# Two-block transformer kernel: 48 modulation units of block 1 leave TensorE and become sums over row tiles on ScalarE, VectorE and GpSimd

## The chip, the core and the metric

The kernel runs on one core of one Trainium2 chip. The metric is the device time of one execution in microseconds (us); the median of three runs is compared. The engines are TensorE (PE; its weight loads are listed as PEld), VectorE (DVE), ScalarE (ACT), GpSimd (POOL) and SyncE (SP), whose queue here only issues the DMAs of the weight stream. Each engine takes its instructions in one fixed order and waits at the first one whose inputs or buffers are not ready.

## The reference

A sequence of 256 tokens with 1024 features passes a first block of two layers (attention, then a gated delta net, each followed by a swiglu feed-forward part) and a second block of two layers. Each layer of the first block is steered by six vectors of 1024 numbers, a vector-matrix product with a weight of its own:

```
cond = jax.nn.silu(c)
for layer in range(DEPTH):
    mod = (cond @ ada_w[layer] + ada_b[layer])[:, None, :]
    shift_m, scale_m, gate_m, shift_f, scale_f, gate_f = jnp.split(mod, 6, axis=-1)
    h = rmsnorm(x, norm_mix_g[layer]) * (1.0 + scale_m) + shift_m
    ...  # mixed = attention (layer 0) or gated delta net (layer 1) of h
    x = x + gate_m * mixed
    h = rmsnorm(x, norm_ffn_g[layer]) * (1.0 + scale_f) + shift_f
    x = x + gate_f * swiglu(h, ffn_w_in[layer], ffn_w_out[layer])
```

The second block has nine such vectors per layer, for two condition vectors (its weight is called `w_mod` in the kernel). "Chunk (l, ch)" below is vector ch of layer l of the first block: 0 and 1 are shift and scale of the mixer, 2 its gate, 3 and 4 shift and scale of the feed-forward part, 5 its gate.

## The kernel before

**The stream.** All weights come through one list of 785 units, `PLAN`, each a tile of 128 rows with up to 1024 columns (512 KB). SP's queue issues their loads in that order, at most 12 units ahead (`pump`). 545 units are matrix weights ("mats"): they land in one of 6 raw buffers, ACT rounds them to a high part (L393), DVE takes the rest as a low part (L394), and PE multiplies both. A product of fp32 data is three matmuls, L420 to L422. With 256 tokens a mat is 24 matmuls.

**The modulation.** The other 240 units are modulation rows: a chunk is eight units (`kt` 0 to 7) of 128 rows each, in a pool of only three buffers, `rawm`. There are two ways to use a unit (`mod_unit`):

- "mod": four small matmuls with the condition as stationary operand (L516, eight instructions in the trace), added up in PSUM over the eight units.
- "acc": the unit, scaled row by row by the condition, is added to a [128, 1024] tile `macc`. Unit 0 is a scaled copy on ACT (L503); every other unit either a multiply-add on DVE (L510) or, in phases which have a tile `mprod`, a scaled copy on ACT into `mprod` (L507) and an add on GpSimd (L508). When all eight are in, `settle` sums `macc` over the partitions with the same four small matmuls.

Both ways end in `mod_end`: a copy on ACT (L533), two transposes on PE (L536), an add on DVE (L544).

**The order.** A scheduler fixes each engine's order at build time, from the program's order and its own estimates; nothing is reordered on the chip. The phases run one after the other: `attn`, `ffn1` (FFN 0), `gdn` (the gated delta net), `ffn1` again (FFN 1), and then the second block. Each phase has its own tiles (`PHASES`). In the feed-forward phases `macc` has two buffers, in `attn` one.

**Entering the gated delta net.** The norm of the new x runs `rsq` (ACT L479, DVE L570 to L572), then for each of eight tiles a multiply on DVE (L639), the high part on ACT (L640) and the low part on DVE (L641). PE then multiplies them, beginning with the mats `ab`, q and k of head 0; each projected head passes a convolution on DVE (L978, out of PSUM). Later four heads at a time go through a triangular inverse, whose tiles `dec` and `m` GpSimd masks (L1025, L1056).

**Which units go which way.** Before the change, of the first block's chunks (0,0) and (0,1) are "mod" units ahead of everything, (0,2) and (0,3) are "acc" units among the attention's mats, (1,0) and (1,1) "acc" units among FFN 0's mats. (0,4), (0,5) are "mod" units between the attention's output mats and behind them, (1,2), (1,3), (1,4) "mod" units among the delta net's mats, and (1,5) stands as eight "mod" units ahead of FFN 1.

Of the kernel before, what the change touches and what calls it, by code (L numbers as in the profile page):

```python
# [12 lines left out]
AF = mybir.ActivationFunctionType  # L13
OP = mybir.AluOpType
AX = mybir.AxisListType

T = 256
# [11 lines left out]

# ---------------------------------------------------------------- weight stream  # L30
# A unit is a [128, n] tile of weights, n <= 1024, made of blocks
# (array, leading index, first row, first column, width).

# [13 lines left out]
def _spread(units, mods, every):  # L47
    """The modulation units one by one between the others: the first three at once."""
    out, mods = mods[:3], mods[3:]
    for i, u in enumerate(units):  # L50
        out.append(u)
        if i % every == every - 1 and mods:
            out.append(mods.pop(0))
    return out + mods


def _evenly(units, mods, a, b, kind="acc"):
    """The modulation units evenly between the units a to b from the end."""
    n = len(units) - a - b
    out, k = [], 0  # L60
    for i, u in enumerate(units):
        out.append(u)
        while k < len(mods) and i >= a + k * n // len(mods):
            out.append((kind,) + mods[k][1:])
            k += 1
    return out
# [30 lines left out]
def plan():  # L97
# [15 lines left out]
    u += _evenly(q, A(0, 2, 3), 4, 0)  # L113
    q = []
# [4 lines left out]
    u += _spread(q, A(0, 4, 5), 1)  # L119
    u += _evenly(_ffn_units(("f", 0), "ffn_w_in", "ffn_w_out", 0), A(1, 0, 1), MODS_IN, MODS_OUT)  # L120
# [6 lines left out]
    u += _evenly(q, A(1, 2, 3, 4), 0, 4, "mod")  # L127
    u += A(1, 5)
    u += _evenly(_ffn_units(("f", 1), "ffn_w_in", "ffn_w_out", 1), B(0, 1, 0), MODS_IN, 2 * MODS_OUT)
# [43 lines left out]
# ---------------------------------------------------------------- small vectors and constants  # L173
# [48 lines left out]
def constants():  # L222
    """Masks, rotations, the DFT and the axial rotation tables: functions of the shapes alone."""
# [66 lines left out]
class Unit:  # L290
    def __init__(self, hi, lo):
# [3 lines left out]
# Tiles of each phase: tag -> (columns, buffers)  # L295
# [3 lines left out]
    "ffn1": {"hb": (KT * 520, 1), "t": (256, 3), "s": (256, 4), "hid": (512, 11), "macc": (1024, 2), "mprod": (1024, 1)},  # L299
# [12 lines left out]
class Builder:  # L312
# [26 lines left out]
    # ---- tiles  # L339
# [34 lines left out]
    # ---- weights  # L374
# [32 lines left out]
    def flush(self, n=len(PLAN)):  # L407
        """The modulation units that stand next in the stream, up to n."""
        end = self.pos + n
        while self.pos < min(end, len(PLAN)) and PLAN[self.pos][0] != "mat":  # L410
            self.pump()
            r = self.raw.pop(self.pos)
            self.mod_unit(PLAN[self.pos][1], r, PLAN[self.pos][0] == "acc")
            self.pos += 1

    def mm3(self, out, u, j, ah, al, start, stop, w=128):
        """out += W[:, block j]^T a"""
# [6 lines left out]
    def mmt(self, out, ah, al, u, j, start, stop, w=512):  # L424
        """out += a^T W[:, block j]"""
# [6 lines left out]
    def gemm(self, u, h, c0, c1, p=None):  # L432
        """One 128-feature tile of a product over the tiles of h, columns c0..c1."""
# [6 lines left out]
    def lead(self, units, h, c0, c1):  # L440
        """The same for some units at once, tile by tile of h as they come."""
# [7 lines left out]
    def pair(self, tag, n):  # L449
        """The two parts of an operand, in one tile or two."""  # L450
# [5 lines left out]
    def split(self, src, hi, lo):  # L456
        """hi + lo = src, each exact in one pass."""
# [4 lines left out]
    def table(self, name):  # L462
        """The scalar engine's table set from here on, in the order of the program."""
# [7 lines left out]
    def after(self, i, j):  # L471
        """Instruction i goes to its engine's queue behind j."""
# [3 lines left out]
    def act(self, out, src, func, **k):  # L476
        """A function of the scalar engine that needs a table."""
# [5 lines left out]
    # ---- modulation  # L483
    def mod_unit(self, key, r, acc):
        """One tile of rows of a modulation's product with the conditions: on the tensor engine, or summed
        over the tiles by a vector engine, so that the tensor engine only sums over the partitions."""
# [13 lines left out]
        for s, a in enumerate(self.macc):  # L500
# [4 lines left out]
            if ns == 1 and "mprod" in self.tags:  # L505
                t = self.t("mprod")
                self.nc.scalar.activation(t, r, AF.Copy, scale=w)  # L507
                self.nc.gpsimd.tensor_tensor(a, a, t, op=OP.add)  # L508
# [10 lines left out]
    def settle(self):  # L519
        """The sums over the partitions that are due."""  # L520
# [30 lines left out]
    def gain(self, name, l, gname, ch):  # L551
        """g * (1 + scale), per stream."""
# [9 lines left out]
    # ---- norms  # L562
    def rsq(self, ss, inv, eps=EPS):
        """(ss * inv + eps) ** -0.5 on [128, 256], one Newton step after the tables' value."""
# [10 lines left out]
    def stats(self, total=KT, gains=None):  # L575
        """Sums of squares of total tiles. With gains, a column offset: of x and, in place of stream 1,
        of x times its gain."""
        return {"gains": gains, "acc": None, "first": {}, "n": {}, "total": total, "p": {}}

    def push(self, st, src, c0, c1):  # L580
        """Squares of one more tile, columns c0..c1. Only the last tile's own sum waits for that tile."""
# [27 lines left out]
    def enter(self, st, ns, A, B, lead):  # L609
        """h = x * r * A + B, split, stream by stream; lead starts on each stream as it is ready."""  # L610
# [9 lines left out]
    def enter_raw(self, st, A, B):  # L620
        """r, and for each tile of x the parts of x * A with those of B as more columns (an even number): of a product over
        them, the columns times r plus the last one are the product over x * r * A + B."""
# [27 lines left out]
    def project_out(self, units, src, ns, gate, st, tail=True):  # L650
        """x += gate * W^T src, tile by tile; the last tiles stream by stream, so that the norm of one
        stream runs beside the products of the other. With one stream, the first tiles at once, so that the
        last of src has time to arrive."""
# [16 lines left out]
    # ---- swiglu  # L670
    def ffn(self, key, st, ns, A, B, gate, more, before_last=None):
        """x += gate * swiglu(x * r * A + B); returns the sums of squares of the new x."""
# [53 lines left out]
    # ---- block 1, layer 0: softmax heads and stick-breaking heads  # L726
# [26 lines left out]
    def vproj(self, key, h):  # L753
        """Values with tokens on the partitions: two tiles [128, 512]."""
# [16 lines left out]
    def headsplit(self, src):  # L771
        """A tile of two heads' rows, each head in its own copy with zeros for the other."""
# [5 lines left out]
    def av(self, pt, v, hp):  # L778
        """Output rows of a pair of heads from their weights [k, (k0 q0, k0 q1, k1 q1)]."""
# [34 lines left out]
    def softmax_rows(self, s, na, scale, P):  # L814
        """P = softmax(scale * s) over the last axis of s [128, na, n]."""
# [49 lines left out]
    def sb_scores(self, qkv, hp):  # L865
        """z = masked scores, e = softplus(z), keys on the partitions."""
# [15 lines left out]
    def sb_weights(self, z, e):  # L882
        """z <- exp(z - what the keys from this one on have taken)."""
# [11 lines left out]
    def scale(self, st, A):  # L895
        """x * r * A, in the columns beside x."""
# [4 lines left out]
    def shift(self, B):  # L901
        """What scale left, plus B, split."""
# [37 lines left out]
    # ---- block 1, layer 1: gated delta rule, the whole sequence as two blocks of 128  # L940
    def gdn_gates(self, h):
        nc = self.nc
        p = self.gemm(self.get(("ab",)), h, 0, T)
        z, e, g = self.t("ga"), self.t("ga"), self.t("ga")
# [36 lines left out]
    def gdn_proj(self, heads, h, out):  # L981
        """Projections of some heads, convolved; a step for each."""
# [24 lines left out]
    def gdn_mats(self, hd, qk, v):  # L1007
        """at, lt [128 s, 3, 128 t]: q k^T and beta k k^T, transposed, with their decays (the first masked
# [583 lines left out]
```

## Time and profile before

| | before |
|---|---|
| device time, median of 3 runs | 2563.02 us (2561.24 to 2563.8) |
| profiled execution, span of the core | 2561.5 us |
| PE busy | 2501.8 us, 98% |
| DVE busy | 1689.1 us, 66% |
| ACT busy | 1128.5 us, 44% |
| POOL busy | 195.9 us, 8% |
| data moved by DMA | 408.38 MB, 159 GB/s mean |

The profiled execution lies inside the range of the timed runs, and its time is its span. The first block takes about the first 745 us of it. Shares of busy time are means over stages with different limits. A matmul's listed duration overlaps the next one's, so the distance between two starts tells what a matmul costs in a stream.

### The profile page before, as it was taken

Reading aid. Unit: us, or ns where it says so; the run is one execution under the profiler, and the core shown is the slowest. Engines: PE = TensorE matmul, PEld = TensorE weight load, DVE = VectorE, ACT = ScalarE, POOL = GpSimd, SP = SyncE. Lnnn points to the kernel's source line nnn. Section 1 sums busy time; section 2 is a strip of 40 time slices with the busy share of each in tenths; the row PEclk is TensorE's granted clock in tenths of the full one; section 3 lists DMA queues with packets and bytes.
Section 4 is the critical chain, followed back from the end, with each engine's and each line's share of the span. In section 5 each row is a group of like instructions: output and inputs, shape, how many; then the busy total and the mean of one; then the engine's idle time right before and its main releaser. Section 6 shows DMA issues by size and latency. Waiting matters only on the chain.

```text
span 2561.5 us, 39957 instructions
## 1 busy us (share of the span) xinstructions
PE 2501.8 (98%) x15915; PEld 2177.1 (85%) x15915; DVE 1689.1 (66%) x2607; ACT 1128.5 (44%) x1955; POOL 195.9 (8%) x183
## 2 busy tenths in 40 slices
PE   6999999999999999999999999999999999999998
PEld 5878998988999887878886888888888888888998
DVE  6857768765887957774646474565656565675665
ACT  4556456565645523233525432323432323555544
POOL 1004100423000100001000100000100000101000
PEclk9999999999999999999999999999999999999999
DMA  8767656324875545663220243454244453232553
GB/s 333 268 209 244 212 188 208 116 83 158 286 248 181 189 160 188 187 197 124 79 79 26 70 154 110 146 175 144 91 159 162 150 178 122 92 109 83 190 183 97
DMA packets 117402, 408.38 MB, mean 159 GB/s; under 512 B 13024, under 2 KB 16352, under 8 KB 117216
## 3 DMA queue, kind: packets, MB, share of 16 engines
q1 hardware_dynamic: 114192, 403.08, 47.8%
q10 hardware_dynamic: 3024, 2.75, 0.4%
q8 instruction: 125, 2.05, 0.3%
q14 instruction: 61, 0.50, 0.1%
HBM read 404.74 MB, written 1.05 MB: 158 GB/s over the span
## 4 chain that ended last, share of the span: by engine, by line
PE 93%; DVE 3%; DMA 2%; ACT 1%; issue 1%; POOL 0%; ACTq 0%; DVEq 0%; SPq 0%
PE pmm L420 25%; PE pmm L422 25%; PE pmm L421 25%; PE pmd L516 2%; PE pax L1389 2%; PE pax L1072 2%; PE pmm L1375 1%; DMA r<-w 1%; PE pax L421 1%; PE pax L422 1%; PE pax L420 1%; PE pax L1385 1%; DVE l L394 1%; PE pnm L607 1%; PE pmm L429 0%
## 5 line engine op out<-in xcount | busy, mean ns | idle before, releaser
L393 ACT CAST h<-r 128x1024 fp32r<-128x1024 f32 (+3 forms) x545 | 550.2, 1016 | 1025.5 <-PE pmm L421 937.6
L394 DVE TENSOR_TENSOR l<-r,h 128x1024 fp32r<-128x1024 f32 (+3 forms) x545 | 658.6, 1213 | 306.0 <-ACT h L393 296.1
L420 PE MATMUL pmm<-h,h 128*128 128x512 f32 (+1 forms) x1928 | 674.3, 351 | 6.7 <-ACT h L640 2.3
L421 PE MATMUL pmm<-h,h 128*128 128x512 f32 (+1 forms) x1928 | 669.1, 348 | 2.0 <-DVE h L641 1.9
L422 PE MATMUL pmm<-h,l 128*128 128x512 f32 (+1 forms) x1928 | 668.9, 347 | 1.0 <-DVE l L394 1.0
L420 PEld LDWEIGHTS pmm<-h,h 128*128 128x128 f32 x1928 | 365.3, 190 | 64.4 <-issue 9.3
L421 PEld LDWEIGHTS pmm<-h,h 128*128 128x128 f32 x1928 | 365.5, 190 | 49.6 <-DVE h L641 3.2
L422 PEld LDWEIGHTS pmm<-h,l 128*128 128x128 f32 x1928 | 365.3, 190 | 47.6 <-DVE l L394 1.5
L420 PE MATMUL pmm<-hid,h 128*128 128x256 f32 (+1 forms) x1053 | 349.5, 332 | 0.0
L422 PE MATMUL pmm<-hid,l 128*128 128x256 f32 (+1 forms) x1053 | 347.5, 330 | 0.3 <-DVE l L394 0.3
L421 PE MATMUL pmm<-hid,h 128*128 128x256 f32 (+1 forms) x1053 | 347.4, 330 | 0.0
L510 DVE SCALAR_TENSOR_TENSOR macc<-r,cond,macc 128x1024 f32<-128x1024 f32 x266 | 330.0, 1281 | 0.3 <-DMA r<-w 0.2
L420 PE MATMUL pmm<-hb,h 128*128 128x258 f32 x1008 | 287.3, 285 | 7.0 <-DVE s L681 6.4
L422 PE MATMUL pmm<-hb,l 128*128 128x258 f32 x1008 | 285.8, 284 | 0.0
L421 PE MATMUL pmm<-hb,h 128*128 128x258 f32 x1008 | 285.3, 283 | 0.0
L420 PEld LDWEIGHTS pmm<-hid,h 128*128 128x128 f32 x1053 | 200.1, 190 | 20.3 <-ACT h L393 1.2
L422 PEld LDWEIGHTS pmm<-hid,l 128*128 128x128 f32 x1053 | 200.1, 190 | 18.7 <-DVE l L394 0.5
L421 PEld LDWEIGHTS pmm<-hid,h 128*128 128x128 f32 x1053 | 200.1, 190 | 18.2
L647 DVE SCALAR_TENSOR_TENSOR x<-pmm,mod_w_mod,x 128x256 f32<-128x256 f32 x188 | 84.6, 480 | 176.5 <-PE pmm L422 176.2
L420 PEld LDWEIGHTS pmm<-hb,h 128*128 128x128 f32 x1008 | 191.6, 190 | 9.8 <-DVE s L681 7.2
L422 PEld LDWEIGHTS pmm<-hb,l 128*128 128x128 f32 x1008 | 192.4, 191 | 0.4 <-issue 0.4
L421 PEld LDWEIGHTS pmm<-hb,h 128*128 128x128 f32 x1008 | 192.4, 191 | 0.3 <-DVE hb L630 0.2
(337 smaller groups left out, 2891.7 us busy)
## 6 DMA issues: line engine op xcount, KB each, us to landing
r<-w SPq DMA_DIRECT2D x665, 512.0 KB, 4.3
r<-w SPq DMA_DIRECT2D x96, 448.0 KB, 3.3
r<-w SPq DMA_DIRECT2D x16, 256.0 KB, 3.0
r<-w SPq DMA_DIRECT2D x8, 384.0 KB, 3.4
const<-const SPq DMA_DIRECT2D x2, 960.0 KB, 6.1
x<-xT ACTq DMA_DIRECT2D x8, 128.0 KB, 4.6
x<-ctxT ACTq DMA_DIRECT2D x8, 128.0 KB, 3.4
out<-x ACTq DMA_DIRECT2D x4, 128.0 KB, 2.1
```

The lines of the kernel that those rows point to most:

```text
L393: nc.scalar.copy(h[:, :n], r[:, :n])
L394: nc.vector.tensor_tensor(lo[:, :n], r[:, :n], h[:, :n].bitcast(F32), op=OP.subtract)
L420: nc.tensor.matmul(out, wh, ah, start=start, stop=False)
L421: nc.tensor.matmul(out, wh, al, start=False, stop=False)
L422: nc.tensor.matmul(out, wl, ah, start=False, stop=stop)
L510: self.nc.vector.scalar_tensor_tensor(a, r, w, a, op0=OP.mult, op1=OP.add)
L516: self.nc.tensor.matmul(p[32 * g:32 * g + 32, :256], w, r[:, 256 * g:256 * g + 256], start=start, stop=stop)
L607: nc.tensor.matmul(p, self.ones, s[:, cg], start=tot == 1, stop=True)
L647: self.nc.vector.scalar_tensor_tensor(v, p[:, s * T - c0:s * T + T - c0], gate[:, 8 * s + m:8 * s + m + 1], v, op0=OP.mult, op1=OP.add)
L1072: nc.tensor.matmul(p[:, s], a[:, s], b[:, s], start=True, stop=True)
L1375: self.nc.tensor.matmul(s, q, k, start=True, stop=True)
L1389: nc.tensor.matmul(o, V[b], pt[:, 128 * b:128 * b + 128], start=b == 0, stop=b == nb - 1)
```

## The change

48 units change from "mod" to "acc": the chunks (0,4), (0,5), (1,2), (1,3), (1,4), (1,5). In the first block 16 "mod" units stay (the two chunks at the start) and 80 are "acc". The positions move with them: (0,2), (0,3), (0,4) stand one behind each mat over the attention's projections and first output mats, (0,5) among the first 16 mats of FFN 0, (1,0) and (1,1) behind those, (1,2) to (1,4) at the same places among the delta net's mats, (1,5) among the first 16 mats of FFN 1, and the first two chunks of the second block a little closer together behind those. From the second block on the order is the same.

The sum for one condition vector is also done in another way in every phase: units 2, 4 and 6 on DVE (L498 of the changed kernel), units 1, 3, 5 and 7 scaled in place on ACT (L495) and added on GpSimd (L496). `mprod` is gone; in the `gdn` phase three tiles are given up for one `macc`. On balance 384 matmul instructions of L516 go and 48 come (six more `settle`); DVE has 16 multiply-adds of 1024 columns more, GpSimd 26 adds more (40 instead of 14), ACT 6 first copies and 26 scalings more.

```
-    u += _evenly(q, A(0, 2, 3), 4, 0)
-    q = []
...
-    u += _spread(q, A(0, 4, 5), 1)
-    u += _evenly(_ffn_units(("f", 0), "ffn_w_in", "ffn_w_out", 0), A(1, 0, 1), MODS_IN, MODS_OUT)
+    u += _evenly(q, A(0, 2, 3, 4), 4, 4)
+    q = _ffn_units(("f", 0), "ffn_w_in", "ffn_w_out", 0)
+    u += _evenly(q[:16], A(0, 5), 2, 3) + _evenly(q[16:], A(1, 0, 1), 0, MODS_OUT)
...
-    u += _evenly(q, A(1, 2, 3, 4), 0, 4, "mod")
-    u += A(1, 5)
-    u += _evenly(_ffn_units(("f", 1), "ffn_w_in", "ffn_w_out", 1), B(0, 1, 0), MODS_IN, 2 * MODS_OUT)
+    u += _evenly(q, A(1, 2, 3, 4), 0, 4)
+    q = _ffn_units(("f", 1), "ffn_w_in", "ffn_w_out", 1)
+    u += _evenly(q[:16], A(1, 5), 2, 3) + _evenly(q[16:], B(0, 1, 0), 0, 2 * MODS_OUT)
...
-            "vb": (256, 4), "dec": (384, 2), "kb": (256, 1), "m": (512, 2), "dt": (512, 3), "d": (512, 2),
-            "y": (512, 2), "uu": (512, 2), "os": (512, 4), "ga": (256, 3)},
+            "y": (512, 2), "uu": (512, 2), "os": (512, 4), "macc": (1024, 1)},
...
-            if ns == 1 and "mprod" in self.tags:
-                t = self.t("mprod")
-                self.nc.scalar.activation(t, r, AF.Copy, scale=w)
-                self.nc.gpsimd.tensor_tensor(a, a, t, op=OP.add)
+            if ns == 1 and kt % 2:
+                self.nc.scalar.activation(r, r, AF.Copy, scale=w)
+                self.nc.gpsimd.tensor_tensor(a, a, r, op=OP.add)
```

The places in the engines' order at which the change is followed below are all at the entry of the delta net.

DVE before, from the end of the chunk (1,1) to the first part of the norm's output (`a` and `r` are the norm's row factor, `t` the first tile of x times it):

```order
L544 TENSOR_TENSOR mod_ada_w_1_4448<-pmd_4445,cols 128x8
L558 SCALAR_TENSOR_TENSOR gain_ada_w_1_4450<-mod_ada_w_1_4448,cols 128x8
L570 TENSOR_TENSOR a_4462<-y_4461 128x256
L571 SCALAR_TENSOR_TENSOR a_4462<-pnm_4431,a_4462 128x256
L572 SCALAR_TENSOR_TENSOR r_4460<-a_4462,r_4460 128x256
L639 SCALAR_TENSOR_TENSOR t_4469<-x_136,gain_ada_w_1_4450,r_4460 128x256
```

DVE after the change, the same place (L558, L559, L560, L627 are the norm's lines now; `r_4230` is unit 2 of chunk (1,2)):

```order
L532 TENSOR_TENSOR mod_ada_w_1_4406<-pmd_4403,cols 128x8
L546 SCALAR_TENSOR_TENSOR gain_ada_w_1_4408<-mod_ada_w_1_4406,cols 128x8
L558 TENSOR_TENSOR a_4420<-y_4419 128x256
L498 SCALAR_TENSOR_TENSOR macc_4523<-r_4230,cond,macc_4523 128x1024
L559 SCALAR_TENSOR_TENSOR a_4420<-pnm_4389,a_4420 128x256
L560 SCALAR_TENSOR_TENSOR r_4418<-a_4420,r_4418 128x256
L627 SCALAR_TENSOR_TENSOR t_4427<-x_136,gain_ada_w_1_4408,r_4418 128x256
```

A multiply-add of the modulation now stands inside the norm's chain. Units 4 and 6 of the same chunk stand further down, ahead of the low parts of the fifth and of the seventh tile (rows not shown).

ACT after the change, behind it (`h_4410` to `h_4417` are the high parts of the eight tiles; `r_4326`, `r_4564` and `r_4717` are units 3, 5 and 7 of chunk (1,2), `h_4599` is the split of a mat); before the change the eight L640 stood in one row with nothing between them:

```order
L492 ACTIVATE macc_4523<-r_4059,cond 128x1024
L468 ACTIVATE y_4419<-pnm_4389,eps1e-06_152 128x256
L468 ACTIVATE y_4419<-y_4419 128x256
L557 ACTIVATE r_4418<-y_4419 128x256
L628 ACTIVATE h_4410<-t_4427,mod_ada_w_0_3358 128x256
L628 ACTIVATE h_4411<-t_4431,mod_ada_w_0_3358 128x256
L495 ACTIVATE r_4326<-r_4326,cond 128x1024
...
L628 ACTIVATE h_4415<-t_4447,mod_ada_w_0_3358 128x256
L495 ACTIVATE r_4564<-r_4564,cond 128x1024
L628 ACTIVATE h_4416<-t_4451,mod_ada_w_0_3358 128x256
L628 ACTIVATE h_4417<-t_4455,mod_ada_w_0_3358 128x256
L495 ACTIVATE r_4717<-r_4717,cond 128x1024
L382 CAST h_4599<-r_4294 128x1024
```

Three scalings that wait for a load now stand among the high parts and ahead of the next split.

PE after the change, where the sums of chunk (1,2) are settled (`pmm_4566` is the last of the first three mats `ab`, q, k of the delta net, `pmm_4603` the fourth); 72 rows lie between the transposes that end chunk (1,1) and this `settle`:

```order
L409 MATMUL pmm_4566<-h_4417,h_4461 128x256
L410 MATMUL pmm_4566<-h_4417,h_4461 128x256
L411 MATMUL pmm_4566<-h_4417,l_4462 128x256
L504 MATMUL pmd_5420<-macc_4523,pick 32x256 x4
L409 MATMUL pmm_4603<-h_4410,h_4519 128x256
```

Before the change three "mod" units stood ahead of these three mats and the others behind them; now PE passes to the fourth mat only when the sum of all eight units is complete. The `settle` of (0,4) stands in the same way 73 rows behind that of (0,3), and that of (1,4) 85 rows behind that of (1,3).

## Rows read from the trace of the kernel before

**Rows 1.** The page, part 1: engine, busy us (share of the span), instructions.

```profile
PE 2501.8 (98%) x15915; PEld 2177.1 (85%) x15915; DVE 1689.1 (66%) x2607; ACT 1128.5 (44%) x1955; POOL 195.9 (8%) x183
```

**Rows 2.** The page, part 4: the chain that ended last, by engine.

```profile
PE 93%; DVE 3%; DMA 2%; ACT 1%; issue 1%; POOL 0%; ACTq 0%; DVEq 0%; SPq 0%
```

**Rows 3.** Timeline of PE: start, us, engine, line, operation, tiles, count [idle before].

```profile
170.77 0.28 PE L422 MATMUL pmm<-og,l 128*128 128x256 f32 x1
170.98 0.64 PE L516 MATMUL pmd<-r,cond 128*32 128x256 f32 x8
171.55 0.38 PE L420 MATMUL pmm<-og,h 128*128 128x256 f32 x1
171.77 0.28 PE L421 MATMUL pmm<-og,h 128*128 128x256 f32 x1
171.89 0.28 PE L422 MATMUL pmm<-og,l 128*128 128x256 f32 x1
```

**Rows 4.** Groups of the modulation's tile on PE, 95 to 760 us: min/median/max ns.

```profile
L516 PE MATMUL pmd<-r,cond x384: 379/379/403, 139.0 to 652.8; 128*32 128x256 f32 x192
```

**Rows 5.** Waits of PE from 100 to 700 us: us in total, times, longest.

```profile
PE pmm L420 <- DVE s L681: 6.4, 2, 5.6
PE pmd L516 <- DMA r<-w: 2.7, 2, 1.5
```

**Rows 6.** Windows: length, busy us of PE, PEld, DVE, ACT, POOL; clock, DMA share, GB/s.

```profile
200.00:235.00 35.00, 28.61 (x221) 28.15 (x220) 32.64 (x36) 20.68 (x37) 12.96 (x5) 0.90 0.68 236
...
220.00:225.00 5.00, 0.54 (x2) 0.55 (x3) 5.00 (x5) 2.42 (x5) 2.85 (x1) 0.67 0.87 281
225.00:230.00 5.00, 5.00 (x31) 5.00 (x30) 3.16 (x6) 2.02 (x4) 0.00 (x0) 0.64 0.73 278
230.00:235.00 5.00, 5.00 (x45) 5.00 (x44) 4.49 (x4) 3.27 (x7) 2.39 (x1) 1.00 0.90 346
...
403.00:440.00 37.00, 36.92 (x310) 33.77 (x308) 31.41 (x51) 23.86 (x37) 0.00 (x0) 1.00 0.74 242
440.00:456.00 16.00, 16.00 (x134) 13.88 (x130) 14.17 (x40) 15.47 (x38) 0.97 (x1) 1.00 0.21 67
```

**Rows 7.** Timeline of DVE in FFN 0.

```profile
210.07 1.21 DVE L394 TENSOR_TENSOR l<-r,h 128x1024 fp32r<-128x1024 f32 x1
...
211.54 0.41 DVE L681 TENSOR_TENSOR s<-pmm,r 128x256 f32<-128x256 f32 x1
211.87 3.38 DVE L394 TENSOR_TENSOR l<-r,h 128x1024 fp32r<-128x1024 f32 x1
215.18 0.41 DVE L681 TENSOR_TENSOR s<-pmm,r 128x256 f32<-128x256 f32 x1
```

**Rows 8.** Timeline of POOL in FFN 0.

```profile
211.77 2.39 POOL L508 TENSOR_TENSOR macc<-macc,mprod 128x1024 f32<-128x1024 f32 x1 [1.91 <-ACT mprod L507]
```

**Rows 9.** Groups of the modulation's sums, whole span: min/median/max ns, first and last start.

```profile
L508 POOL TENSOR_TENSOR macc<-macc,mprod x14: 2384/2409/3214, 193.6 to 263.6; 128x1024 f32<-128x1024 f32 x14
...
L503 ACT ACTIVATE macc<-r,cond x40: 1133/1150/1179, 40.8 to 2108.9; 128x1024 f32<-128x1024 f32 x40
...
L510 DVE SCALAR_TENSOR_TENSOR macc<-r,cond,macc x266: 1270/1278/1760, 48.3 to 2130.8; 128x1024 f32<-128x1024 f32 x133
```

**Rows 10.** The page, part 6: DMA issues, KB each, median us to landing.

```profile
r<-w SPq DMA_DIRECT2D x665, 512.0 KB, 4.3
```

**Rows 11.** Timeline of PE at the entry of the delta net.

```profile
389.72 1.50 PE L516 MATMUL pmd<-r,cond 128*32 128x256 f32 x24 [0.26 <-DVE mod_ada_w L544]
392.69 0.62 PE L420 MATMUL pmm<-h,h 128*128 128x256 f32 x3 [1.47 <-ACT h L640]
```

**Rows 12.** Timeline of ACT at the same entry.

```profile
388.60 0.37 ACT L533 COPY meada_w<-pmd 128x256 f32<-128x256 f32 x1 [0.52 <-PE pmd L516]
```

**Rows 13.** Timeline of DVE at the same entry.

```profile
390.62 0.42 DVE L571 SCALAR_TENSOR_TENSOR a<-pnm,a 128x256 f32<-128x256 f32 x1
...
398.25 0.89 DVE L641 SCALAR_TENSOR_TENSOR h<-t,mod_ada_w,h 128x256 fp32r<-128x256 f32 x2 [0.18 <-ACT h L640]
```

More of the change, by code (lines that the diff above doesn't have):

```diff
@@ L44, in _rows @@
     return ("mat", key, [(name, l, k * 128, m * 128, 128) for k in range(k0, k1)])
[L47 to L54, printed above, removed]
 def _evenly(units, mods, a, b, kind="acc"):
@@ L298 @@
              "macc": (1024, 1), "sm": (512, 2), "e": (768, 1), "pt": (768, 1), "tab": (512, 1), "t": (256, 2)},
-    "ffn1": {"hb": (KT * 520, 1), "t": (256, 3), "s": (256, 4), "hid": (512, 11), "macc": (1024, 2), "mprod": (1024, 1)},
[2 rows of a table removed]
+    "ffn1": {"hb": (KT * 520, 1), "t": (256, 3), "s": (256, 4), "hid": (512, 11), "macc": (1024, 2)},
[2 rows of a table added]
             "vb": (256, 4), "dec": (384, 2), "kb": (256, 1), "m": (512, 2), "dt": (512, 3), "d": (512, 2),
[1 row of a table removed]
[1 row of a table added]
     "mix": {"h": (512, 18), "t": (256, 2), "raw": (512, 6), "tmp": (512, 4), "o": (512, 8), "pt": (512, 4), "ru": (256, 1)},
@@ L943, in gdn_gates @@
         p = self.gemm(self.get(("ab",)), h, 0, T)
-        z, e, g = self.t("ga"), self.t("ga"), self.t("ga")
+        z, e, g = self.t("vb"), self.t("vb"), self.t("vb")
         dt, al = COLS["dt"][0], COLS["a_log"][0]
```

4 rows, old and new, of the table PHASES are left out of this document.

## The prediction

> **What bounds the kernel now.** The page's first part says it: PE is busy 98% of the span, DVE 66%, POOL 8% [rows 1]. The chain that ended last is PE's work for 93% of its length [rows 2]. So time is won by taking instructions from PE, as long as no other engine makes it wait. The modulation units are such instructions, and the timeline of PE gives their price. Of the stream of matmuls with 256 columns, one starts every 0.12 us (171.77 to 171.89). Between the L422 that starts at 170.77 and the L421 at 171.77 stand one unit and two steps of the stream, so the unit costs 1.00 - 0.24 = 0.76 us [rows 3]. All 48 units that move lie between 139 and 653 us (384 instructions) [rows 4].
>
> Then the waits. In the stretch that the change touches PE waits little: 6.4 us for the scaled products of FFN 0 (5.6 of it at once) and 2.7 us for units that had not landed [rows 5]. The 5.6 us cost more than their length: in the windows the granted clock is 0.67 while PE waits and 0.64 in the next five us, where PE starts 31 matmuls and not 45, about 1.7 us lost, and full again after 230 [rows 6]. Of TensorE's two levels, 1.2 and 2.4 GHz, it had the lower one for most of that stretch, after standing still.
>
> Last, the engines that receive the work. DVE's timeline in FFN 0 shows a split L394 of 1.21 us, and one of 3.38 us [rows 7]. The long one began 0.10 us after a GpSimd add of 2.39 us had [rows 8]. It lost 2.17 us, that is, it ran when the add was over. L681 beside it reads PSUM and stayed at 0.41 us.
>
> **What goes.** 48 units at 0.76 us are 36.5 us. Nine of them earn nothing: three groups of three stand where PE waits for a norm anyway. At the delta net's entry PE does 24 instructions and still waits 1.47 us for the first part of h [rows 11]; the other two groups are at 178 and at 638 us. That takes 6.8 us off. Six new sums over partitions (settle) are the same four matmuls and cost 6 x 0.76 = 4.6 us. Copy, transposes and bias stay. Net: -25.1 us. PE's waits for units (2.7 us [rows 5]) go with the units that were loaded in a burst: -2.7. The same burst held up the mats' loads ahead of FFN 0, and the splits, then stretched by adds, were late until 224 us. Wait and clock are 5.6 + 1.7 = 7.3 us. Now no burst is there, but the first sixteen mats of FFN 0 carry four adds and three multiply-adds of chunk (0,5), where before DVE was 32.6 of 35 us busy [rows 6]. Between nothing and 7.3 I take half: -4.
>
> **What comes, where it waits.** An "acc" chunk is a chain, since every step writes macc: one copy on ACT (1.15), four adds (2.41 each) and three multiply-adds (1.28) [rows 9], 14.6 us, and units 3 to 7 must first be loaded into a buffer that an earlier unit has left, 4.3 us from issue [rows 10], the odd ones also scaled (taken as the copy's 1.15).
>
> I follow it at the delta net's entry. The copy of chunk (1,1) ends at 388.97 [rows 12]; behind it ACT does unit 0, to 390.1; the add of unit 1 ends at 392.5, unit 2 on DVE at 393.8. That multiply-add stands in DVE's queue ahead of the norm's second step, which ran at 390.62 before [rows 13]: **the whole entry is 3.2 us late**. Unit 3: its buffer is free at 390.1, landed 394.4, scaled 395.6, added 398.0. Unit 4: done 399.3. Unit 5: free 393.8, landed 398.1, scaled 399.3, added 401.7. Unit 6: free 398.0, landed 402.3, done 403.6; behind it on DVE stand the last two low parts, ready at 404.5 where they were at 399.1. Unit 7: free 399.3, landed 403.6, scaled 404.8, added 407.2. Only then can PE settle and go on to its fourth mat. Before, its 72 matmuls from 392.69 on [rows 11] took 8.6 us, to 401.3 if nothing waited. So PE is 6 us late, not a mere 4.6 us of instructions. The lower bound is the 3.2 us, the upper 6 plus one more landing, 10.3, if unit loads queue on SP behind mats. I take 6, and 2 for the clock after the gap (nearest row: the 1.7 above).
>
> The same chain is 407.2 - 388.6 = 18.6 us from a settle to the next where a chunk follows in the same buffer. (0,4) has 73 matmuls of PE in that time, 36 of them with 512 columns: at 0.24, 0.12 and 0.06 us by their columns, some 11.5 us. The bounds are 0 (PE waits there for attention weights as well, so that time passes anyway) and 7; I take 5. (1,4) has 85 matmuls, some 8 us, but between links of the triangular inverse, which spread them out: between 0 and 10.6, I take 3. The three settles together: 16 us with the clock.
>
> **What comes, in DVE's time.** In 403 to 456 us DVE is busy 45.6 of 53 us and PE 52.9 [rows 6]; PE loses some eight units, 6 us. DVE gains three multiply-adds (3.8 us) and meets four adds. They can block it 4 x 2.17 = 8.7 us, or nothing if they always fall beside convolutions, which read PSUM; the two ends are 49.4 and 58.1 us, against 47 for PE. Half blocked, DVE needs 53.7. As splits run ahead during the wait at the settle, I take 4 us, and 2 for FFN 1's first mats, where (1,5) puts four more adds. In the attention DVE has room. ACT at 44% [rows 1] costs by order alone, which is counted above.
>
> The Trainium skill, SBUF — State Buffer, section "Who interferes with whom", says that a VectorE instruction with two inputs in SBUF and a GpSimd instruction that reads SBUF exclude each other for the whole instruction, and that one with at most one SBUF input goes free. Rows 7 and 8 agree, 3.38 beside 0.41 us. By it all adds that meet a split cost it the full length; the rival on blocking below is what that would make.
>
> **The sum.** -25.1 - 2.7 - 4 + 16 + 6 = -9.8 us. The profiled span is 2561.5, and its time is 1.5 below the median of the three runs, 2563.0. Against the median: **2553 us**.
>
> **Rivals.** *All of it is won.* Nothing waits longer at a settle, and DVE keeps up: -25.1 - 2.7 - 4 = -31.8, about 2531 us. For it speaks that DVE is at 66% [rows 1]; against it the chain just followed, made of measured durations. Chance 0.15.
>
> *Blocking eats it.* Every add costs a split its 2.17 us where DVE is nearly full. In the delta net DVE then needs 58.1 - 47 = 11 us more than PE (7 above my 4), FFN 0 keeps its late splits (4), FFN 1 loses 2 more: -9.8 + 13 = +3.2, about 2566, no change that can be told. It decides where more than half of the adds meet a split. Chance 0.17.
>
> *Slower: loads at the head of SP's queue.* A chunk's load waits on SP until a buffer is given back by ACT, POOL or DVE, and mats queue behind it; a chunk's load issued late delays the chain by one landing, and there are two links of buffers in it (unit 3 for unit 0's, then unit 6 for unit 3's). If each costs 4.3 us more at each of the three settles, 26 us are added: -9.8 + 26 = +16, about 2579. It decides from 3.3 us per settle on. For it: SP has one queue, and three buffers for such units. Against: mats are loaded far ahead, and the page's DMA rows show a median of 4.3 us, waits for the queue aside. Chance 0.23, together with smaller sums above +5 us.
>
> **How the numbers follow.** My forecast, -5 to -18 us (2545 to 2558), has 0.45. 0.2% is 5.1 us, about what a measurement of this kernel can tell from no change. Faster by more: 0.45 + 0.15 and some of the boundary cases lost, 0.58; within: 0.18; slower: 0.24. The range leaves out the far half of the first rival and the far half of the last: 2534 to 2572.
>
> **What would show it.** Right: L504 with the condition is gone after 100 us; the norm's second step at the delta net's entry starts some 3 us later behind its copy, and PE stands still ahead of the settle of (1,2); shorter gaps ahead of those of (0,4) and (1,4); the clock falls behind the longest gap; adds on POOL in pairs with splits near 3.4 us; the second block unchanged to 0.1%. Wrong: no gap ahead of the three settles (then the chain is shorter than I make it, and the first rival holds), waits of PE for L383 in 400 to 460 us longer than at the settle (the second), or SP's loads of mats landing after PE wants them (the third).

## The result and the profile after

The changed kernel is slower: 2582.31 us (median of four runs, 2581.09 to 2583.81) beside 2562.90, a ratio of 1.0076 with a 95% interval of 1.0062 to 1.0090, some 19.4 us. The forecast was 2553 us, faster, and its range ended at 2572; both are wrong. Where a run of before is compared below, it ran on the same chip as the experiment. Experiments are also compared with each other across chips; the medians of the kernel before lie between 2562.8 and 2564.1 us on them, so a difference of a us or two between such runs tells nothing.

The page's first part and the chain by engine of the changed kernel:

```profile
span 2582.0 us, 39454 instructions
PE 2487.2 (96%) x15579; PEld 2179.5 (84%) x15579; DVE 1736.9 (67%) x2623; ACT 1159.3 (45%) x1987; POOL 258.8 (10%) x209
...
PE 84%; DVE 7%; issue 3%; ACT 2%; DMA 2%; POOL 1%; DVEq 0%; SPq 0%; ACTq 0%; POOLq 0%
```

PE has 14.6 us less work than in [rows 1], in a span 20.5 us longer. The chain passes through DVE for 7% and not 3% [rows 2]. PE's waits from 100 to 700 us, us in total, times, longest, are a new list; the two rows of [rows 5] shrank or are gone:

```profile
PE pax L1021 <- DVE kb L1018: 8.0, 3, 4.5
PE pmm L409 <- ACT h L628: 7.1, 2, 6.4
PE pnm L595 <- DVE a L559: 5.5, 3, 2.2
PE pmm L409 <- DVE s L669: 4.7, 6, 1.5
PE pmm L409 <- ACT hb L617: 3.0, 2, 1.9
```

They name the norm at the delta net's entry (L628), the normalization of its heads (L559), the heads' matrices that are built ahead of the inverse (L1018) and FFN 0 and 1. None is a settle.

The stages tell more than the sum. Each starts with the first matmul of its kind in PE's timeline (attention scores, scaled products of an FFN, projections of the delta net):

| stage, us | before | after | forecast of the change | measured |
|---|---|---|---|---|
| to the first attention scores | 127.0 | 136.3 | 0 | +9.3 |
| to FFN 0 | 54.7 | 47.7 | about -2 | -7.0 |
| FFN 0 and the delta net's entry | 211.1 | 210.8 | about -4 | -0.3 |
| delta net, to FFN 1 | 247.8 | 263.9 | about -2 | +16.1 |
| FFN 1 and all behind it | 1921.0 | 1923.4 | about -2 | +2.4 |

The forecast column puts the terms of the prediction's sum into the stages where the units and settles stand in the two timelines. The settle of (0,4), at 149.7 us, is in the second row with its 5 us; of the 6 us that PE was to be late at the settle of (1,2), 3.2 are in the third row.

Most of the loss is PE standing still in the delta net: of its 263.9 us PE is busy 238.6, where it was 244.2 of 247.8. So it stands still for 25.3 us and not 3.6.

The entry of the delta net, where the prediction followed the chain step by step. First DVE, then GpSimd (start, us, engine, line, operation):

```profile
389.71 1.85 DVE L558 TENSOR_TENSOR a<-y 128x256 f32<-128x256 f32 x1 [1.00 <-ACT y L468]
391.49 1.27 DVE L498 SCALAR_TENSOR_TENSOR macc<-r,cond,macc 128x1024 f32<-128x1024 f32 x1
392.69 0.41 DVE L559 SCALAR_TENSOR_TENSOR a<-pnm,a 128x256 f32<-128x256 f32 x1
...
396.59 2.71 DVE L629 SCALAR_TENSOR_TENSOR h<-t,mod_ada_w,h 128x256 fp32r<-128x256 f32 x2 [0.18 <-ACT h L628]
...
402.00 2.99 DVE L627 SCALAR_TENSOR_TENSOR t<-x,gain_ada_w,r 128x256 f32<-128x256 f32 x2
404.92 1.27 DVE L498 SCALAR_TENSOR_TENSOR macc<-r,cond,macc 128x1024 f32<-128x1024 f32 x1
406.12 0.87 DVE L629 SCALAR_TENSOR_TENSOR h<-t,mod_ada_w,h 128x256 fp32r<-128x256 f32 x2
```

```profile
388.95 2.34 POOL L496 TENSOR_TENSOR macc<-macc,r 128x1024 f32<-128x1024 f32 x1 [5.51 <-ACT macc L492]
396.21 2.41 POOL L496 TENSOR_TENSOR macc<-macc,r 128x1024 f32<-128x1024 f32 x1 [4.93 <-ACT r L495]
401.75 2.57 POOL L496 TENSOR_TENSOR macc<-macc,r 128x1024 f32<-128x1024 f32 x1 [3.13 <-DVE h L629]
406.66 2.59 POOL L496 TENSOR_TENSOR macc<-macc,r 128x1024 f32<-128x1024 f32 x1 [2.34 <-DVE h L629]
```

As forecast, the multiply-add stands ahead of the norm's second step. That step starts at 392.69 and the last low part ends at 407.0, where it was 390.62 and 399.1 [rows 13], though everything ahead ended 1.1 us earlier. So the step is 3.2 us late, as forecast, and the low part 9.0 us, where 5.4 were forecast. Not forecast: the first three of these adds also hold up the norm's own steps beside them. L558 takes 1.85 us, where the same step (L570) took 0.43, and pairs that took 0.89 and 0.88 us take 2.71 and 2.99. Then PE, at the head of the projections and at the settle:

```profile
394.75 0.80 PE L409 MATMUL pmm<-h,h 128*128 128x256 f32 x2 [6.44 <-ACT h L628]
...
409.31 0.64 PE L504 MATMUL pmd<-macc,pick 128*32 128x256 f32 x8
```

PE stands still for the norm, and the settle itself waits for nothing. With this gap of 6.44 us the granted clock falls: it is 0.62 in 390 to 400 and 0.86 and 0.83 in the next two windows of 10 us. From 395 to 402 us PE starts a matmul of 256 columns every 0.21 us and not every 0.12: it has the lower of its two levels, 1.2 and 2.4 GHz. Some 45 us into the stage DVE is full, and PE waits for what it does next; windows of busy us (PE, PEld, DVE, ACT, POOL; clock):

```profile
440.00:450.00 10.00, 9.96 (x77) 9.55 (x76) 10.00 (x13) 6.06 (x10) 2.38 (x1) 1.00 0.82 269
450.00:460.00 10.00, 6.11 (x44) 5.51 (x44) 9.79 (x20) 9.98 (x22) 2.40 (x1) 1.00 0.64 227
460.00:470.00 10.00, 3.92 (x19) 3.21 (x19) 9.85 (x27) 5.11 (x14) 0.97 (x1) 0.71 0.01 2
```

In the attention the softmax waits. First its step L825 before, then the same step after (L813), both min/median/max ns; last one pair of such steps, and the add that it met:

```profile
L825 DVE TENSOR_SCALAR pz<-pz,s x16: 275/312/347, 79.2 to 97.5; 128x128 f32<-128x128 f32 x8, 128x256 f32<-128x256 f32 x8
```

```profile
L813 DVE TENSOR_SCALAR pz<-pz,s x16: 274/341/2354, 83.5 to 107.4; 128x128 f32<-128x128 f32 x8, 128x256 f32<-128x256 f32 x8
...
97.18 2.34 DVE L813 TENSOR_SCALAR pz<-pz,s 128x256 f32<-128x256 f32 x2
...
96.72 2.38 POOL L496 TENSOR_TENSOR macc<-macc,r 128x1024 f32<-128x1024 f32 x1 [7.51 <-DVE s L811]
```

### The profile page after: what moved, and what is told of

Its sections match the earlier page's. It is cut to its first block, busy times and chain, and to the rows that moved or that the text cites. A ratio compares the mean times of both kernels' runs of the same rounds, so it can differ in the third digit from the quotient of the medians.

```text
span 2582.0 us, 39454 instructions
## 1 busy us (share of the span) xinstructions
PE 2487.2 (96%) x15579; PEld 2179.5 (84%) x15579; DVE 1736.9 (67%) x2623; ACT 1159.3 (45%) x1987; POOL 258.8 (10%) x209
## 4 chain that ended last, share of the span: by engine, by line
PE 84%; DVE 7%; issue 3%; ACT 2%; DMA 2%; POOL 1%; DVEq 0%; SPq 0%; ACTq 0%; POOLq 0%
PE pmm L409 23%; PE pmm L410 23%; PE pmm L411 23%; DVE l L383 2%; PE pax L1060 2%; DMA r<-w 2%; PE pax L1377 2%; PE pmm L1363 1%; PE pax L410 1%; PE pax L411 1%; PE pax L409 1%; PE pmd L504 1%; PE pax L1373 1%; DVE macc L498 1%; ACT h L382 1%
## 5 line engine op out<-in xcount | busy, mean ns | idle before, releaser
L383 DVE TENSOR_TENSOR l<-r,h 128x1024 fp32r<-128x1024 f32 (+3 forms) x545 | 671.0, 1236 | 290.1 <-ACT h L382 279.8
L498 DVE SCALAR_TENSOR_TENSOR macc<-r,cond,macc 128x1024 f32<-128x1024 f32 x282 | 352.9, 1288 | 11.6 <-POOL macc L496 7.6
L409 PEld LDWEIGHTS pmm<-hid,h 128*128 128x128 f32 x1053 | 200.4, 190 | 21.9 <-issue 1.7
L410 PEld LDWEIGHTS pmm<-hid,h 128*128 128x128 f32 x1053 | 200.4, 190 | 18.2
```

Source lines behind the costliest of these rows:

```text
L383: nc.vector.tensor_tensor(lo[:, :n], r[:, :n], h[:, :n].bitcast(F32), op=OP.subtract)
L409: nc.tensor.matmul(out, wh, ah, start=start, stop=False)
L410: nc.tensor.matmul(out, wh, al, start=False, stop=False)
L498: self.nc.vector.scalar_tensor_tensor(a, r, w, a, op0=OP.mult, op1=OP.add)
```

## The experiments

Two theories stood against each other. A: the adds on GpSimd cost, since each keeps DVE out while it runs. B: DVE's load and the place of the sums in the engines' order cost, whoever adds. In every kernel the scheduler orders anew, so an edit moves other instructions a little too.

**Which stage: the delta net's units back on TensorE.**

```
-    u += _evenly(q, A(1, 2, 3, 4), 0, 4)
+    u += _evenly(q, A(1, 2, 3, 4), 0, 4, "mod")
```

> The changed kernel with the 24 units of chunks (1,2), (1,3), (1,4) back as matmuls on TensorE, at the same places; everything else as changed. Theory A (the delta net's stage is where the time went: VectorE is the engine that ends last there, by the added multiply-adds and by adds of GpSimd that block it): the stage from the first mat of the delta net to FFN 1 shrinks from 264 us to about the 248 of before, the norm at its entry is back by 3 us, and the kernel takes 2562 to 2567 us. Rival B (the loss is made in the attention and only shows later, since loads stay late): the delta net stays at 264 us and the kernel within 5 us of 2582.

2563.74 us, ratio to before 1.0004 (0.9995 to 1.0014). The stage comes back to 248.1 us and the entry's delay goes (projections start at 390.0). The rival falls: with the delta net's units on TensorE 18.6 of the 19.4 us are gone. The attention's 9 us stay (scores at 136.8), which the 7 us won behind them and the earlier norm offset.

**Who adds: everything on VectorE.**

```
-            if ns == 1 and kt % 2:
-                self.nc.scalar.activation(r, r, AF.Copy, scale=w)
-                self.nc.gpsimd.tensor_tensor(a, a, r, op=OP.add)
-            else:
-                self.nc.vector.scalar_tensor_tensor(a, r, w, a, op0=OP.mult, op1=OP.add)
+            self.nc.vector.scalar_tensor_tensor(a, r, w, a, op0=OP.mult, op1=OP.add)
```

> The changed kernel with units 1, 3, 5, 7 of every one-condition chunk as multiply-adds on VectorE too (no scaling on ScalarE, no add on GpSimd). Theory A1 (blocking by GpSimd's adds is the larger cost; an add stretches a VectorE instruction by up to 2.17 us and a multiply-add takes 1.28): 2565 to 2575 us, with the splits back at 1.21 us and the softmax steps of the attention at their old length. Rival A2 (VectorE's plain load is the cost; 40 multiply-adds more are 51 us of its time): 2585 to 2600 us.

2555.15 us, ratio 0.9974 (0.9965 to 0.9984): faster than before, and 27 us faster than the changed kernel, though DVE does 40 multiply-adds more. That is better than either theory expected. Its page:

```profile
PE 2479.3 (97%) x15579; PEld 2172.5 (85%) x15579; DVE 1729.7 (68%) x2663; ACT 1118.1 (44%) x1947; POOL 166.2 (7%) x169
```

DVE's busy time falls from 1736.9 to 1729.7 us, with 40 x 1.28 = 51 us more to do. So the 40 adds had lengthened DVE's instructions by about 58 us, 1.5 us for each. The longest split in the first 760 us falls from 3.41 to 1.75 us. Four stages gain: 6.6 us up to the scores, 10.3 in FFN 0 with the entry, 5.6 in the delta net, 5.5 behind; from the scores to FFN 0 it is 0.6 longer. The delta net still takes 258.2 us, 10.5 more than before.

**The place of the chunk at the entry.**

```
-    u += _evenly(q, A(1, 2, 3, 4), 0, 4)
+    u += _evenly(q, A(1, 2, 3, 4), 7, 4)
```

> The changed kernel with the chunks (1,2) to (1,4) spread from the 8th mat of the delta net on instead of from the first, so that no step of a sum should stand inside the norm at its entry. If the place of chunk (1,2) inside that norm is a cost of its own: the first mat starts about 3 us and the last part of h about 9 us earlier behind the settle of (1,1), and the kernel takes 2570 to 2575 us. Rival (VectorE's time is short in the whole first half of the delta net, wherever the steps stand): the entry is faster, the stretch to the first inverse as much slower, 2579 to 2585 us.

2578.60 us, ratio 1.0064 (1.0047 to 1.0081). The edit didn't do what it was for: from the last low part's end at 410.6 and the settle at 412.9 one sees that the scheduler still put the whole chunk (1,2) into the entry. It tells nothing about the place.

**The odd units left out.**

```
             if ns == 1 and kt % 2:
-                self.nc.scalar.activation(r, r, AF.Copy, scale=w)
-                self.nc.gpsimd.tensor_tensor(a, a, r, op=OP.add)
+                continue
```

> The changed kernel with units 1, 3, 5, 7 of each one-condition chunk loaded but left out of the sum (the modulation of block 1 is then wrong by these rows): no scaling on ScalarE and no add on GpSimd. It shows what those 80 instructions cost in all. If they make the loss: 2550 us or less, since PE's saving is kept. If the multiply-adds on VectorE and the chain's place make it: 2570 us or more.

2542.46 us, ratio 0.9926 (0.9911 to 0.9941): 40 us below the changed kernel. The 80 instructions of ScalarE and GpSimd are the whole loss and more; the same 40 units as multiply-adds cost 13. Most of these 13 are in the delta net: its stage takes 247.1 us here, 258.2 with the multiply-adds and 263.9 in the changed kernel.

**The kernel before without its 14 adds.**

```
-            if ns == 1 and "mprod" in self.tags:
-                t = self.t("mprod")
-                self.nc.scalar.activation(t, r, AF.Copy, scale=w)
-                self.nc.gpsimd.tensor_tensor(a, a, t, op=OP.add)
-            else:
-                self.nc.vector.scalar_tensor_tensor(a, r, w, a, op0=OP.mult, op1=OP.add)
+            self.nc.vector.scalar_tensor_tensor(a, r, w, a, op0=OP.mult, op1=OP.add)
```

> The kernel of before with its 14 scaled adds of FFN 0 (ScalarE and GpSimd) as multiply-adds on VectorE; nothing else. Theory A1 (blocking by GpSimd's adds is what costs): FFN 0 shrinks by 5 to 10 us, since the 5.6 us that TensorE waits there were made by splits of 3.4 us, and the kernel takes 2553 to 2558 us. Rival A2 (VectorE's load): 14 multiply-adds are 18 us more of it in a stage where it is nearly full, so 2563 to 2570 us.

2553.33 us, ratio 0.9960 (0.9945 to 0.9974). The 10 us come out of FFN 0 with the entry (200.4 us beside 211.1). PE's waits from 100 to 700 us:

```profile
PE pax L1058 <- DVE dt L1091: 1.8, 1, 1.8
PE pmm L420 <- ACT h L635: 1.5, 1, 1.5
PE pnm L601 <- DVE acc L594: 1.1, 1, 1.1
PE pmd L511 <- DMA r<-w: 0.7, 1, 0.7
```

The 5.6 us of [rows 5] are gone with the adds, and the clock's loss with them (1.00 from 215 to 235 us), while the burst of "mod" units ahead of FFN 0 is still there. So the burst alone doesn't make that wait; it needs the adds.

**Scaled on ScalarE, added on VectorE.**

```
-                self.nc.gpsimd.tensor_tensor(a, a, r, op=OP.add)
+                self.nc.vector.tensor_tensor(a, a, r, op=OP.add)
```

> The changed kernel with units 1, 3, 5, 7 still scaled in place on ScalarE, but added on VectorE. It parts the scaling and its place in ScalarE's queue from the add on GpSimd. If GpSimd's adds are the cost: 2553 to 2560 us, as with multiply-adds. If the scalings between ScalarE's other work are a good part of it: 2565 us or more.

2559.50 us, ratio 0.9983 (0.9973 to 0.9992). Against the changed kernel 23 of the 27 us come back by moving the add alone. The scalings between ScalarE's other work go with the remaining 4, which are not clear of noise: the interval overlaps that of the multiply-adds.

**Both edits together.** Multiply-adds as in the second experiment, the delta net's units on TensorE as in the first.

> The changed kernel with both: units 1, 3, 5, 7 as multiply-adds on VectorE, and the delta net's 24 units back on TensorE. If the two losses are separate, the stage of the delta net comes down from 258 us (multiply-adds alone) to the 248 of before and the rest stays: 2543 to 2547 us. If GpSimd's adds were the whole loss and the sums as such cost nothing in the delta net, the 24 units on TensorE make it no faster than 2553 us.

2542.92 us, ratio 0.9920 (0.9905 to 0.9935), with 247.9 us for the delta net, at the edge of what separate losses were expected to give. By themselves the two edits bring back 18.6 and 27.2 us, together 39.4: the 6 us between are mostly counted twice, since the first edit also takes away the delta net's twelve adds (5.6 us of the second). But for that the two losses are separate. What the change meant to do works in the attention and the FFNs, when VectorE adds.

**The add in four pieces.**

```
-                self.nc.gpsimd.tensor_tensor(a, a, r, op=OP.add)
+                for c in range(0, 1024, 256):
+                    self.nc.gpsimd.tensor_tensor(a[:, c:c + 256], a[:, c:c + 256], r[:, c:c + 256], op=OP.add)
```

> The changed kernel with each add of GpSimd cut into four of 256 columns. If one add keeps VectorE out for its whole length and the length of one instruction matters, splits of 3.4 us go to under 2 us each and the kernel gains some 5 to 15 us: 2567 to 2577 us. If VectorE loses the same time in all, since it is kept out by each of the four: within 4 us of 2582, or slower.

2581.72 us, ratio to before 1.0065 (1.0048 to 1.0082), no different from the changed kernel. The splits of the first 760 us, and the pieces (min/median/max ns):

```profile
L383 DVE TENSOR_TENSOR l<-r,h x185: 677/1218/1794, 35.0 to 757.8; 128x1024 fp32r<-128x1024 f32 x153, 128x896 fp32r<-128x896 f32 x16, 128x512 fp32r<-128x512 f32 x16
...
L497 POOL TENSOR_TENSOR macc<-macc,r x160: 714/740/2367, 48.9 to 700.5; 128x256 f32<-128x256 f32 x160
```

The pages of this kernel, part 1 and its multiply-adds (busy us, mean ns, idle time before them), and the multiply-adds of the changed kernel:

```profile
PE 2493.4 (97%) x15579; PEld 2182.7 (85%) x15579; DVE 1710.8 (66%) x2623; ACT 1158.7 (45%) x1987; POOL 308.6 (12%) x329
...
L499 DVE SCALAR_TENSOR_TENSOR macc<-r,cond,macc 128x1024 f32<-128x1024 f32 x282 | 353.0, 1289 | 31.6 <-POOL macc L497 25.8
```

```profile
L498 DVE SCALAR_TENSOR_TENSOR macc<-r,cond,macc 128x1024 f32<-128x1024 f32 x282 | 352.9, 1288 | 11.6 <-POOL macc L496 7.6
```

No split there exceeds 1.79 us any more, and DVE is busy 26 us less than in the changed kernel (1710.8 beside 1736.9), yet the time is the same. The pieces wait too: four of them beside splits took 4.98 us together in FFN 0, and DVE now stands still for GpSimd's part of the sum for 25.8 us and not 7.6. So 18 of the 26 us come back as waits inside the chain.

**Where the sums should stand in the delta net.** All multiply-adds on VectorE; first the chunks from the 8th mat on (the edit of the third experiment), then only (1,4) as a sum, then (1,3) and (1,4):

```
+    u += [("acc",) + x[1:] if x[0] == "mod" and x[1][2] in (4,) else x
+          for x in _evenly(q, A(1, 2, 3, 4), 0, 4, "mod")]
```

> All multiply-adds on VectorE (2555 us), and the chunks (1,2) to (1,4) spread from the 8th mat of the delta net on, so that the norm at its entry should hold no step of a sum. If the place in the norm makes most of the 12 us that the sums still cost in the delta net against matmuls (2555 beside 2543): the last part of h is ready within 11 us of the settle of (1,1), as before, and the kernel takes 2544 to 2549 us. If VectorE's time in the projections makes it: 2552 to 2557 us.

> The fastest so far (2543 us: multiply-adds on VectorE, the delta net's units on TensorE) with chunk (1,4) alone as a sum. It stands in the second half of the delta net, where VectorE was busy only some 60% of the time before. If the loss of the sums sits in the entry and the projections, with (1,2) and (1,3): 2537 to 2543 us, since eight units at 0.76 us less one settle are 5.3 us of TensorE. If each chunk costs alike (12 us over three): 2546 to 2548 us.

> The same with chunks (1,3) and (1,4) as sums and only (1,2) on TensorE. If the entry's chunk (1,2) makes the loss: 2533 to 2543 us. If the projections of the first heads with (1,3) do, where VectorE is busy 86% before: 2548 us or more.

2546.99 us (ratio 0.9934, 0.9918 to 0.9951), 2541.58 us (0.9911, 0.9896 to 0.9926) and 2549.99 us (0.9945, 0.9930 to 0.9959). The first lands where a place inside the norm would have put it (2544 to 2549), but not by that mechanism: the last part of h is ready at 387.0 us, 17 us behind the settle of (1,1) and not 11. In its timeline of DVE the sums still stand in the norm, one behind each step:

```profile
371.19 1.28 DVE L494 SCALAR_TENSOR_TENSOR macc<-r,cond,macc 128x1024 f32<-128x1024 f32 x1 [0.19 <-ACT macc L492]
372.39 0.42 DVE L554 TENSOR_TENSOR a<-y 128x256 f32<-128x256 f32 x1
372.73 1.28 DVE L494 SCALAR_TENSOR_TENSOR macc<-r,cond,macc 128x1024 f32<-128x1024 f32 x1
373.92 0.42 DVE L555 SCALAR_TENSOR_TENSOR a<-pnm,a 128x256 f32<-128x256 f32 x1
```

The chunk (1,4) alone as a sum shortens the delta net to 244.1 us from 247.9, but the whole kernel by only 1.3 us, and the two intervals overlap. With (1,3) as well it is 255.1 us, and the time is in the range that put the loss into the projections with (1,3). Both chunks together cost where one does not, and with all three sums from the 8th mat on it is 250.1 us. What goes with the dearer ones is the settle of (1,4): three of its four matmuls at 565 to 575 us, inside the second triangular inverse, in the two kernels with 255 and 258 us, all four at 603 to 610 us, behind it, in those with 244 and 250. That is an observation, and the third experiment speaks against it as the whole cause: there the settle stands at 642 us, behind that inverse, and the stage takes 261.9 us, with adds on GpSimd worth some 6. No run sets the place of that settle by itself, so the cause stays open.

**Adds that nobody needs.** The sums on VectorE, and behind units 1, 3, 5, 7 an add that doubles the used unit in its own buffer:

```
             self.nc.vector.scalar_tensor_tensor(a, r, w, a, op0=OP.mult, op1=OP.add)
+            if ns == 1 and kt % 2:
+                self.nc.gpsimd.tensor_tensor(r, r, r, op=OP.add)
```

> All sums as multiply-adds on VectorE (2555 us), and behind units 1, 3, 5, 7 an add of GpSimd that nobody reads: it doubles the used unit in its own buffer (no scaling on ScalarE, no link of the sum's chain on GpSimd). The result stays that of the reference. If GpSimd's adds cost by keeping VectorE out, whoever needs their result: splits near 3.4 us come back, and the kernel takes 2575 to 2595 us. If they cost since each link of the chain is handed from engine to engine (ScalarE, GpSimd, VectorE): 2555 to 2562 us.

2591.67 us, ratio to before 1.0107 (1.0090 to 1.0123): 36.5 us more than the same kernel without them, 0.9 us for each. With the same instructions DVE is busy 1774.6 us and not 1729.7, 1.1 us more for each add. Splits and adds (the first row min/median/max ns, the second busy us, mean ns and what ended the idle time before):

```profile
L383 DVE TENSOR_TENSOR l<-r,h x181: 678/1218/2934, 35.1 to 758.9; 128x1024 fp32r<-128x1024 f32 x149, 128x896 fp32r<-128x896 f32 x16, 128x512 fp32r<-128x512 f32 x16
...
L496 POOL TENSOR_TENSOR r<-r 128x1024 f32<-128x1024 f32 x40 | 93.2, 2331 | 227.0 <-DVE macc L494 187.3 <-DVE s L805 18.8 <-issue 12.3
```

No link of a sum is on GpSimd here and no scaling on ScalarE, yet the loss is larger than the 27 us. So the loss doesn't need a chain handed from engine to engine. The buffers of the odd units do stay in use some 2.4 us longer, which this run doesn't part from the blocking; it can't lengthen a split. A third way, GpSimd's own sums and masks coming late behind the adds, doesn't show: from 30 to 780 us DVE waits 6.8 us here for the norm's partial sums and the masks of `dec`, 6.3 in the changed kernel and 8.4 before.

## Why the prediction was wrong

**The step that failed** is the one headed "What comes, in DVE's time". It put all cost of the adds at 4 us in the delta net and 2 in FFN 1, with the words "In the attention DVE has room"; and of FFN 0's 7.3 us it took half as won while chunk (0,5) put adds there. Measured, moving all adds to VectorE is worth 27 us, 23 of them by the add alone. The error was not the price of one block, read rightly from [rows 7, 8] as up to 2.17 us: the 40 adds lengthened DVE's instructions by 1.5 us each. It was to ask where DVE's busy share is near full. In these traces a block also cost where PE waits for the next thing DVE does, in the norm and in the softmax. In the attention that made +9.3 us where nothing was forecast, of which 6.6 come back with the adds on VectorE.

**A second miss: the sums in the delta net, whoever adds.** The sum has about -2 us for that stage, and about -6 without the 4 us for DVE's time. With no add on GpSimd it measured +10.5, and PE stood still there for 20.1 us, where it was 3.6 before. The prediction put PE's waits there mostly at the settles; the longest that the list of that run names in the stage is for DVE's work on the heads (4.2 us for the line that was L1018). With the odd units left out the stage is back at 247.1 us, so the steps of the sums cost there. Whether they do so by DVE's time or by their place in the chain, no run parts.

**The rival on blocking had the mechanism and not the size.** It gave +3.2 us, since it counted the delta net and the FFNs only and left the norm's steps and the attention out. The rule of the Trainium skill that was weighed (SBUF — State Buffer, "Who interferes with whom") pointed the right way, and was read too narrowly. In the Trainium skill the same section lists `tensor_scalar` among the operations that may take a mode in which they contend too. Here the L813 with one SBUF tile as input took 2.35 us where 0.35 was the longest before; which mode it took, no run shows. The 0.41 us of L681, set against the long split in the prediction, show little, since both rows of [rows 7] lie at the edges of an add. A better row is an L647, also with one input in PSUM: 0.48 us at 249.26, wholly inside the add from 247.31 to 249.72 us, and 0.48 is its usual length.

**Right: what goes.** From the scores to FFN 0 ten units that cost time go and one settle comes, -6.8 us by the prediction's prices, and the measured change is -7.0. The worth of the whole shows where nothing blocks: the kernel with sums on VectorE outside the delta net takes 2543 us beside 2553 for that of before with its own adds on VectorE.

**Right in place, short in size: the entry.** The multiply-add inside the norm, the settle at 409.3 (407.2 was worked out), DVE's last low part at 407.0 (404.5), PE's stand-still and the lower clock came as told, though the settle of (1,1) was 1.1 us earlier. Adds are not needed for most of PE's wait for the first h: it is 1.5 us before and 6.4 in the changed kernel, and 5.4 with no add of the sums on GpSimd, where two multiply-adds stand inside the norm.

**Wrong: waits at the settles of (0,4) and (1,4)**, 5 and 3 us of the sum. PE's only wait for GpSimd's sums in the first 780 us is 0.7 us, at the settle of (0,4); at that of (1,4) it has none. In the settle of (1,2) the wait had been taken upstream, by the norm.

**The last rival**, loads at the head of SP's queue, ended near the measured time, 2579 us, by a mechanism that the runs don't show. With the adds on VectorE the same units are loaded and the kernel is 27 us faster; PE's waits from 100 to 700 us name no load, and ScalarE's splits wait for loads 1.5 us in all from 30 to 780 us. What does wait for loads are the scalings, 19.3 us, and those cost some 4 us by the sixth experiment. Its time is luck. So is it that the change without the adds comes to 2555 us, near the 2553 that was predicted: the sum held 6 us for DVE's time with the adds, and 8 us for two settles where PE hardly waited, and these stand against what was missed in the delta net.

## What to carry to other kernels

An instruction on GpSimd isn't free because GpSimd idles: read the length of VectorE's instructions beside it, and charge the stretch wherever TensorE waits for VectorE next, here in the norms and the softmax. Before moving work from TensorE to a chain over three engines, try the chain on one of them alone: here the plain multiply-add on VectorE won by 27 us, and taking 14 adds out of the old kernel won 10. The fastest kernels of the study, 2541.6 and 2542.9 us, keep sums out of the first half of the delta net and off GpSimd.

## What was not expected of the hardware

GpSimd's add held up a VectorE instruction with one SBUF tile (L813, from at most 0.35 to 2.35 us). Adds were held up too: one beside splits took 3.99 us, where the median is 2.40. And cutting the adds into four took 26 us off VectorE's busy time and nothing off the kernel's.
